# Four early steps of the output projection ahead of a norm's sums, and GpSimd's convolution additions behind the last key write, in a two-layer attention and convolution encoder

## The chip, the cores and the metric

The kernel runs on one core of a Trainium2 chip. The core has five engines that run their own instruction queues, each in order: TensorE (PE, matrix products, with its weight loads shown as PEld), VectorE (DVE), ScalarE (ACT), GpSimd (POOL) and SyncE (SP, which here only issues DMAs). They meet through semaphores. The metric is the device time of one execution in microseconds; lower is better.

## The reference

Two layers of an encoder over 512 tokens of 1024 features, in float32. Only the mixing part in the middle of a layer is touched by the change.

```python
for l in range(DEPTH):                       # 2 layers
    x = x + 0.5 * swiglu(rms_norm(x, ffn1_norm[l]), ...)
    h = rms_norm(x, mix_norm[l])
    p = h @ w_in[l]
    attn = mla_group(p[..., :o_kv], ...)     # 8 heads: q and k per head normalised, 96 wide; block-causal softmax
    conv = conv_group(p[..., o_cv:], ...)    # u = a * sigmoid(g); causal depthwise conv of 31 taps over 512 channels;
                                             # layer norm over the channels; silu
    x = x + jnp.concatenate([attn, conv], axis=-1) @ w_out[l]
    x = x + 0.5 * swiglu(rms_norm(x, ffn2_norm[l]), ...)
    x = rms_norm(x, post_norm[l])
```

## The kernel before

All activations stay in SBUF with features on partitions: x is eight tiles of 128 x 512. Float32 accuracy in the big products comes from splitting each operand into a high and a low part; `mm3` (L170 to L172) issues three matmuls for one product of 128 x 128 weights with 128 x 512 values. The feed-forward parts take most of the time; the change lies in `mix_body`, once per layer.

**Order of the work.** A scheduler places the instructions on the engines from the order in which the code is written; `tc.issue_after(i)` forbids that what follows is placed ahead of i, and `tc.high_priority` brings a block forward. What stands on one engine then runs in that order. Waits between engines are only for data and for buffers.

**Keys.** `keys` takes four tiles of 128 tokens. For each it scales the key of every head by an inverse root that GpSimd works out (`rsqrt`, L189) and writes the two parts of `kn` on VectorE (L820 and L822; L819 scales the factor of the second). `order["keys"]` holds GpSimd's last inverse root. `turn` then transposes queries and keys on TensorE (L848, L853). The first four weight tiles of the output projection (`wo`) are loaded behind `order["keys"]`: their low parts come by a DMA that GpSimd issues (L155).

**Convolution.** Four tiles of 128 channels. Tile 0 and tile 3 are summed on VectorE (L968), 31 taps each. For the other two, ScalarE makes one product per tap into one of four buffers `pr` (L972), and GpSimd adds it to the tile's sum `ys[c]` (L974). For taps from PAUSE = 16 on, and for the second of these tiles, the addition is placed behind `order["keys"]`; these are thirty in a layer. Part of the third tile's taps run on TensorE (L676).

**Attention.** For each head: scores on TensorE (L872), row maxima on VectorE (L876), exponentials on ScalarE (L880), transposes of the probabilities (L895), copies out of PSUM (L898), and for each pair of heads the value products (L917) and their scaling (L920), which `split` makes into an operand of the output projection (L177, L178). ScalarE's exponentials and its products for the convolution are in one queue.

**The norm and the output projection.** The four channel tiles are summed, centred (L1001), squared on ScalarE (L200, L203) and added up on VectorE (L207). TensorE forms the sums per token (`sums`, L214), VectorE and GpSimd make the inverse root, and TensorE spreads it over the partitions (`spread`, L233). Only then are the convolution's tiles scaled (L1016), put through silu (L1018) and split (L177, L178). TensorE needs them as operands 4 to 7 of the projection; operands 0 to 3 are the four pairs of heads. So products with the heads' operands are put around sums and spread as early steps, a step being one operand for one of four output tiles, three matmuls:

```python
steps = [(m, k) for m in range(WOG) for k in range(3)] + [(m, 3) for m in range(WOG)]
...
early_steps(0, EA, heads[H - 1][EARLY])
...
early_steps(EA, EB, sums)
early_steps(EB, len(steps), spreading)
```

With EA = 2 and EB = 6 two of the sixteen steps may come behind the last head's scores, four behind the sums, and ten behind the spread.

Of the kernel before, what the change touches and what calls it, by code (L numbers as in the profile page):

```python
# [12 lines left out]
ALU = mybir.AluOpType  # L13
# [7 lines left out]
NT = S // P  # L21
H = 8
DN = 64
DR = 32
DQ = DN + DR
# [25 lines left out]
GLUP = 0  # L51
EARLY = "s"
PRELOAD = 1
EA = 2
EB = 6
WOG = 4
CHAIN = 400
WAKE = 10
# [20 lines left out]
def encoder_kernel(ctx: ExitStack, tc: tile.TileContext, xT, consts, vecs, rgain, wgu1, wd1, wdq1,  # L79
# [11 lines left out]
    def nm(s):  # L91
        uid[0] += 1
        return f"{s}{uid[0]}"
# [4 lines left out]
    def tmp(w=S, dt=FP):  # L98
        return tmps.tile([P, w], dt, tag="t", name=nm("t"))
# [13 lines left out]
    def tiny(tag, w, dt=FP):  # L113
        return small.tile([P, w], dt, tag=tag, name=nm(tag))

    V, A, G, T = nc.vector, nc.scalar, nc.gpsimd, nc.tensor
# [15 lines left out]
    minus_half = cpool.tile([P, H], FP, name="minus_half")  # L132
# [10 lines left out]
    def vv(l, name):  # L143
        o, w = VOFF[name]
        return vec[:, l, o:o + w]

    def load_w(src, w, kind=""):
        raw = wpool.tile([P, WC], FP, tag="raw", name=nm("raw"), bufs=3)
        nc.sync.dma_start(out=raw[:, :w], in_=src)
        hi = wpool.tile([P, WC], FR, tag="wh", name=nm("wh"))  # L150
        order["cast"] = A.copy(hi[:, :w], raw[:, :w]).ins  # L151
        lo = low()
        if kind == "sum":
            A.activation(lo[:, :w], raw[:, :w], AF.Copy, scale=-1.0)
            G.dma_start(out=lo[:, :w], in_=src, accum_op=ALU.add)  # L155
            return hi, lo
        (G if kind in POOLW.split() else V).tensor_tensor(lo[:, :w], raw[:, :w], hi[:, :w].bitcast(FP),  # L157
                                                          ALU.subtract)
        return hi, lo
# [4 lines left out]
    order = {}  # L164
# [22 lines left out]
    def rsqrt(y, ve):  # L187

        return G.tensor_tensor(y, ve, minus_half[:, 0:y.shape[1]], ALU.pow).ins  # L189
# [439 lines left out]
    def mix(l, gx, norm, done):  # L629
        with tc.tile_pool(name="k", bufs=4) as kpool:  # L630
            mix_body(kpool, l, gx, norm, done)

    def mix_body(kpool, l, gx, norm, done):
        u, order = [], {}
# [53 lines left out]
        kn = kpool.tile([P, NT, H, DQ], FP, tag="kn", name=nm("kn"), bufs=1)  # L688
# [109 lines left out]
        def up_kv(w, t, n=S):  # L798

            ts_ = slice(t * P, (t + 1) * P)  # L800
            ps = bank()
            for k in range(2):
                cs = slice(k * n, (k + 1) * n)
                mm3(ps, ckT[k][0][:, ts_], ckT[k][1][:, ts_], w[0][:, cs], w[1][:, cs], k == 0, k == 1)
            return ps

        def keys():
            wk = load_w(wkv[l, 0], WC, "uk")
            for t in range(NT):
                ps = up_kv(wk, t)  # L810
                A.copy(kn[:, t, :, 0:DN], ps.rearrange("p (h d) -> p h d", h=H))
                j = tmp()
                A.activation(j, ps, AF.Square)
                V.tensor_reduce(ssk[:, t], j.rearrange("p (h d) -> p h d", h=H), axis=AX.X, op=ALU.add)
                V.tensor_scalar(ssk[:, t], ssk[:, t], ckc[:, t:t + 1], None, ALU.add)
                sck = small.tile([P, H], FP, tag="sck", name=nm("sck"))
                order["keys"] = rsqrt(sck, ssk[:, t])
                scp = small.tile([P, H], FP, tag="scp", name=nm("scp"))
                V.tensor_scalar(scp, sck, ratio[:, t:t + 1], None, ALU.mult)  # L819
                V.tensor_tensor(kn[:, t, :, 0:DN], kn[:, t, :, 0:DN],  # L820
                                sck[:, :, None].to_broadcast([P, H, DN]), ALU.mult)
                V.tensor_tensor(kn[:, t, :, DN:DQ], cke[:, t, None, :].to_broadcast([P, H, DR]),  # L822
                                scp[:, :, None].to_broadcast([P, H, DR]), ALU.mult)


        first = groups([wcv[l, 0], wcv[l, 1]], gx)
# [157 lines left out]
        def early_steps(a, b, behind_):  # L984
            with tc.issue_after(behind_):
                for m, k in steps[a:b]:
                    if k == 0:
                        early.append(bank())
                    group(early[m], wo[m], at, (k,), KD)

        early_steps(0, EA, heads[H - 1][EARLY])
        st = Stats()
# [14 lines left out]
        if PRELOAD:  # L1007
            with behind(heads[H - 1]["exps"]):
                A.activation(tiny("pre", 1), ysum[:, 0:1], AF.Silu)
        early_steps(EA, EB, sums)  # L1010
        early_steps(EB, len(steps), spreading)
        lg, lb = vv(l, "lg"), vv(l, "lb")
# [283 lines left out]
```

## Time and profile before

| | us |
|---|---|
| three runs | 1794.69, 1797.07, 1797.32 (median 1797.07) |
| profiled execution, its own time | 1794.2 |
| its span, first to last instruction | 1792.4 |
| PE busy | 1778.5 (99%) |
| DVE busy | 1493.5 (83%) |
| ACT busy | 1093.8 (61%) |
| POOL busy | 382.1 (21%) |
| PE's wait for L207 ahead of the sums, both layers | 2.8 |
| PE's wait for the last keys (L822), both layers | 1.1 |

The granted TensorE clock is 1.00 throughout. In the first layer the keys are written from about 432 to 444 us of the span, attention runs from 445 to about 507, sums and spread stand at 508 and 512; the second layer repeats it some 888 us later. A row of a timeline gives the start, the length, the engine, the line, the operation, its output and inputs, how often it stands there in a row, and in brackets the idle time of the engine ahead of it and what ended it. In a row with several instructions the length is that from the start of the first to the end of the last.

### The profile page before, as it was taken

To read this page: it belongs to the slowest core of one execution; us is meant where nothing else is said; L and a number is where in the kernel's file an instruction comes from. 1 tells how busy PE (TensorE), PEld (TensorE's weight loads), DVE (VectorE), ACT (ScalarE), POOL (GpSimd) and SP (SyncE) were. 2 spreads that over 40 slices of the span, in tenths; PEclk is the share of its full clock that TensorE was granted. 3 is DMA by queue.
4 is the path that set the end of the run, shared out by engine and by line. 5 is a ranking of instruction groups with operands and counts; after the bars stand their busy time and mean duration, and the time that the engine had idled before them with its cause. 6 is when DMAs were issued, how large, how long until landed. Compare 5 with 4: busy or idle time off the path is not lost.

```text
span 1792.4 us, 29441 instructions
## 1 busy us (share of the span) xinstructions
PE 1778.5 (99%) x11430; PEld 1579.1 (88%) x11430; DVE 1493.5 (83%) x2309; ACT 1093.8 (61%) x1699; POOL 382.1 (21%) x313
## 2 busy tenths in 40 slices
PE   9999999999999999999999999999999999999998
PEld 7899999888678899999888999998976788999997
DVE  7898988689965989898779989876999568989883
ACT  5565756467853575756645757564778435756564
POOL 1000000248722000000310000002585310000002
PEclk9999999999999999999999999999999999999999
DMA  5657575324213466665426575743260126575742
GB/s 170 171 131 182 136 178 123 109 84 127 68 28 96 124 166 162 153 160 131 124 65 171 123 194 122 193 114 111 81 157 21 52 79 170 130 185 131 183 117 74
DMA packets 71947, 228.28 MB, mean 127 GB/s; under 512 B 8448, under 2 KB 9600, under 8 KB 71808
## 3 DMA queue, kind: packets, MB, share of 16 engines
q1 hardware_dynamic: 55536, 171.87, 30.5%
q0 software_dynamic: 16128, 54.53, 18.2%
q8 instruction: 89, 1.46, 0.3%
q14 instruction: 50, 0.41, 0.1%
q10 hardware_dynamic: 144, 0.00, 0.0%
HBM read 222.19 MB, written 2.10 MB: 125 GB/s over the span
## 4 chain that ended last, share of the span: by engine, by line
PE 90%; DVE 6%; ACT 1%; issue 1%; DMA 1%; POOL 0%; SPq 0%; ACTq 0%; DVEq 0%
PE ps L170 24%; PE ps L171 23%; PE ps L172 23%; PE ps L389 11%; PE ps L390 6%; DVE cv L968 1%; DVE mx L876 1%; DMA raw<-in_wgu 1%; PE ps L917 1%; DVE r L898 0%; PE ps L895 0%; PE ps L214 0%; DVE r L855 0%; PE ps L676 0%; DVE wl L262 0%
## 5 line engine op out<-in xcount | busy, mean ns | idle before, releaser
L171 PE MATMUL ps<-r,wh 128*128 128x256 f32 (+1 forms) x2556 | 812.9, 319 | 0.1
L170 PE MATMUL ps<-r,wh 128*128 128x256 f32 (+1 forms) x2556 | 811.0, 320 | 1.1 <-ACT wh L151 0.5
L172 PE MATMUL ps<-r,wl 128*128 128x256 f32 (+1 forms) x2364 | 755.3, 321 | 0.0
L170 PEld LDWEIGHTS ps<-r,wh 128*128 128x128 f32 x2556 | 483.8, 189 | 45.6 <-ACT wh L151 3.7
L171 PEld LDWEIGHTS ps<-r,wh 128*128 128x128 f32 x2556 | 484.6, 190 | 36.4 <-DVE r L178 1.5
L172 PEld LDWEIGHTS ps<-r,wl 128*128 128x128 f32 x2364 | 448.2, 190 | 33.8
L389 PE MATMUL ps<-xj,wh 128*128 128x512 f32 x864 | 303.8, 391 | 0.0
L151 ACT CAST wh<-raw 128x1024 fp32r<-128x1024 f32 (+3 forms) x148 | 132.6, 901 | 216.9 <-PE ps L171 135.3
L260 ACT CAST wh<-fr 128x1024 fp32r<-128x1024 f32 (+1 forms) x160 | 157.8, 986 | 103.8 <-DVE fr L426 49.3
L406 POOL DMA_DIRECT2D ls<-in_wgu x72 | 62.5, 868 | 734.5 <-ACT ls L405 525.0
L157 DVE TENSOR_TENSOR wl<-raw,wh 128x1024 fp32r<-128x1024 f32 (+3 forms) x132 | 141.2, 1077 | 91.0 <-ACT wh L151 90.3
L262 DVE TENSOR_TENSOR wl<-fr,wh 128x1024 fp32r<-128x1024 f32 (+1 forms) x160 | 181.8, 1136 | 20.1 <-ACT wh L260 20.1
L389 PEld LDWEIGHTS ps<-xj,wh 128*128 128x128 f32 x864 | 161.4, 188 | 30.1
L390 PE MATMUL ps<-xj,ls 128*128 128x256 f32 x576 | 161.3, 280 | 0.0
L974 POOL TENSOR_TENSOR y<-y,pr 128x495 f32<-128x495 f32 (+29 forms) x90 | 121.7, 1353 | 46.4 <-ACT pr L972 41.0
L260 ACT CAST wh<-raw 128x1024 fp32r<-128x1024 f32 (+1 forms) x100 | 98.1, 981 | 45.2 <-PE ps L171 24.5
L262 DVE TENSOR_TENSOR wl<-raw,wh 128x1024 fp32r<-128x1024 f32 (+1 forms) x100 | 113.3, 1133 | 14.2 <-ACT wh L260 13.8
L390 PEld LDWEIGHTS ps<-xj,ls 128*128 128x128 f32 x576 | 108.3, 188 | 0.0
L405 ACT ACTIVATE ls<-fr 128x1024 fp32r<-128x1024 f32 (+1 forms) x56 | 56.1, 1002 | 75.9 <-PE ps L390 42.8
L207 POOL TENSOR_TENSOR r<-r,t 128x512 f32<-128x512 f32 x45 | 73.3, 1638 | 136.5 <-ACT t L203 136.2
L968 DVE SCALAR_TENSOR_TENSOR cv<-m,vec,cv 128x511 f32<-128x511 f32 (+14 forms) x120 | 87.8, 732 | 3.8 <-ACT cv L964 2.2
L406 POOL DMA_DIRECT2D ls<-in_wdq x32 | 27.6, 863 | 262.1 <-ACT ls L405 262.1
(257 smaller groups left out, 2919.1 us busy)
## 6 DMA issues: line engine op xcount, KB each, us to landing
fr<-in_wgu SPq DMA_DIRECT2D x112, 512.0 KB, 4.3
ls<-in_wgu POOLq DMA_DIRECT2D x72, 512.0 KB, 6.3
raw<-in_wgu SPq DMA_DIRECT2D x62, 512.0 KB, 4.6
fr<-in_wdq SPq DMA_DIRECT2D x48, 384.0 KB, 5.0
ls<-in_wdq POOLq DMA_DIRECT2D x32, 384.0 KB, 4.8
raw<-in_wd SPq DMA_DIRECT2D x32, 384.0 KB, 3.2
raw<-in_wd SPq DMA_DIRECT2D x32, 256.0 KB, 2.8
raw<-in_wcv SPq DMA_DIRECT2D x16, 512.0 KB, 3.6
```

The costliest lines, as they stand in the source:

```text
L151: order["cast"] = A.copy(hi[:, :w], raw[:, :w]).ins
L157: (G if kind in POOLW.split() else V).tensor_tensor(lo[:, :w], raw[:, :w], hi[:, :w].bitcast(FP), ALU.subtract)
L170: T.matmul(o, lh, rh, start=first, stop=False, skip_group_check=free)
L171: T.matmul(o, lh, rl, start=False, stop=False, skip_group_check=free)
L172: order["mm"] = T.matmul(o, ll, rh, start=False, stop=last, skip_group_check=free).ins
L260: A.copy(hi[:, :w], src[:, :w])
L262: order["lo"] = V.tensor_tensor(lo[:, :w], src[:, :w], hi[:, :w].bitcast(FP), ALU.subtract).ins
L389: T.matmul(o, w[0][:, c], both, start=start and k == 0, stop=False, skip_group_check=True)
L390: last = T.matmul(o[:, 0:HS], w[1][:, c], both[:, 0:HS], start=False, stop=k == 3, skip_group_check=True).ins
L406: G.dma_start(out=lo[:, :n], in_=w, accum_op=ALU.add)
L968: V.scalar_tensor_tensor(acc[:, s:], u[c][:, :S - s], tap(k), acc[:, s:], ALU.mult, ALU.add)
L974: order["conv"] = G.tensor_tensor(ys[c][:, s:], ys[c][:, s:], pr[:, s:], ALU.add).ins
```

## The change

`EA` goes from 2 to 4 and `EB` from 6 to 8: four early steps may be placed ahead of the sums, four again between sums and spread, and eight behind the spread. In `keys`, a new product of one column follows the loop over the tiles on GpSimd: it reads the last column of `kn` of the last tile and writes a buffer of one column. `order["keys"]` now names this product, so that the weight loads and the thirty additions are placed behind it. Lines behind L822 move by two: the additions are L976 in the changed kernel, the last heads' scaling L922.

```diff
-EA = 2
-EB = 6
+EA = 4
+EB = 8
...
                 V.tensor_tensor(kn[:, t, :, DN:DQ], cke[:, t, None, :].to_broadcast([P, H, DR]),
                                 scp[:, :, None].to_broadcast([P, H, DR]), ALU.mult)
+            order["keys"] = G.tensor_tensor(tiny("pre", 1), kn[:, NT - 1, H - 1, DQ - 1:DQ], minus_half[:, 0:1],
+                                            ALU.mult).ins
```

The three places of the programs that the prediction rests on are the sums on VectorE, the sums on TensorE, and the first additions on GpSimd. On GpSimd, ahead of the additions (y) behind the last key scale (sck), it stood before:

```order
L189 TENSOR_TENSOR sck_4559<-ssk_3863,minus_half 128x8
L155 DMA wl_5393<-in_wout 128x1024
L974 TENSOR_TENSOR y_3848<-y_3848,pr_5496 128x496
L155 DMA wl_5400<-in_wout 128x1024
L974 TENSOR_TENSOR y_3848<-y_3848,pr_5499 128x495
```

and now:

```order
L189 TENSOR_TENSOR sck_4559<-ssk_3863,minus_half 128x8
L824 TENSOR_TENSOR pre_4565<-kn_3856,minus_half 128x1
L155 DMA wl_5395<-in_wout 128x1024
L155 DMA wl_5402<-in_wout 128x1024
L976 TENSOR_TENSOR y_3848<-y_3848,pr_5498 128x496
L976 TENSOR_TENSOR y_3848<-y_3848,pr_5501 128x495
```

The new product stands ahead of two weight loads and of the additions. On VectorE, where the squares of the convolution's channels (m) are added and the last heads' output (t) is scaled, it stood before:

```order
L207 TENSOR_TENSOR m_4633<-m_4633,m_3846 128x512
L920 TENSOR_TENSOR t_5383<-ps_5374,t_5372 128x512
L207 TENSOR_TENSOR m_4633<-m_4633,m_4058 128x512
L178 TENSOR_TENSOR r_5386<-t_5383,r_5385 128x512
L221 TENSOR_SCALAR vtok_5642<-cv_5643 128x4
```

and now:

```order
L207 TENSOR_TENSOR m_4635<-m_4635,m_3846 128x512
L207 TENSOR_TENSOR m_4635<-m_4635,m_4058 128x512
L922 TENSOR_TENSOR t_5385<-ps_5376,t_5374 128x512
L178 TENSOR_TENSOR r_5388<-t_5385,r_5387 128x512
L221 TENSOR_SCALAR vtok_5651<-cv_5652 128x4
```

The last addition of squares stands ahead of the scaling. On TensorE, from the last value product (ps_5374, now ps_5376) over the sums (L214) to the next steps, before:

```order
L917 MATMUL ps_5374<-r_5346,m_4801 64x128
L214 MATMUL cv_5643<-ones,m_4633 128x1 x4
L170 MATMUL ps_5619<-r_5357,wh_5391 128x512
L171 MATMUL ps_5619<-r_5358,wh_5391 128x512
L172 MATMUL ps_5619<-r_5357,wl_5393 128x512
```

and now:

```order
L919 MATMUL ps_5376<-r_5348,m_4803 64x128
L170 MATMUL ps_5621<-r_5359,wh_5393 128x512
L171 MATMUL ps_5621<-r_5360,wh_5393 128x512
L172 MATMUL ps_5621<-r_5359,wl_5395 128x512
L171 MATMUL ps_5631<-m_5159,wh_5400 128x512
L172 MATMUL ps_5631<-m_5158,wl_5402 128x512
L214 MATMUL cv_5652<-ones,m_4635 128x1 x4
```

The two steps stand between the value products and the sums, but for their sixth matmul (L170 of ps_5631), which stands ahead of the value products. The orders on PE, DVE, ACT and POOL around the attention differ in further places, and SyncE's is the same.

## The prediction

> **What bounds the kernel now.** I read the page first: the span, the busy times and the chain.
>
> ```profile
> span 1792.4 us, 29441 instructions
> PE 1778.5 (99%) x11430; PEld 1579.1 (88%) x11430; DVE 1493.5 (83%) x2309; ACT 1093.8 (61%) x1699; POOL 382.1 (21%) x313
> PE 90%; DVE 6%; ACT 1%; issue 1%; DMA 1%; POOL 0%; SPq 0%; ACTq 0%; DVEq 0%
> ```
>
> TensorE (PE) is busy for 1778.5 of 1792.4 us and carries 90% of the chain. No multiplication leaves the program, so a gain comes out of the 13.9 us in which TensorE stands still, or out of a stretch where another engine paces it. Next, the windows of the first layer's attention and of what follows it (columns behind the length: PE, its weight loads, DVE, ACT, POOL, the granted clock, DMA):
>
> ```profile
> 445.00:500.00 55.00, 54.48 (x446) 35.34 (x446) 54.02 (x101) 47.32 (x117) 37.06 (x30) 1.00 0.26 65
> 500.00:530.00 30.00, 28.62 (x138) 21.34 (x135) 16.76 (x25) 14.33 (x23) 5.07 (x3) 1.00 0.02 4
> ```
>
> From 445 to 500 VectorE (DVE) works 54.02 of 55.00 us and paces the stage. From 500 to 530 TensorE has 1.38 us without work. The view of TensorE's waits (total, times, longest) names that gap, and one more:
>
> ```profile
> PE cv L214 <- DVE m L207: 2.8, 2, 1.4
> PE ps L853 <- DVE kn L822: 1.1, 2, 0.9
> ```
>
> The change touches both: 2.8 us ahead of the two norms' sums and 1.1 us ahead of the transposes of the last keys, 3.9 us or 0.22% of the span.
>
> **Part 1: four steps ahead of the sums.** The timeline of the first layer around the sums:
>
> ```profile
> 504.38 2.37 PE L917 MATMUL ps<-r,m 128*64 128x512 f32 x14
> 508.13 1.05 PE L214 MATMUL cv<-ones,m 128*128 128x1 f32 x8 [1.38 <-DVE m L207]
> 516.93 0.39 PE L170 MATMUL ps<-r,wh 128*128 128x512 f32 x1
> ...
> 517.61 0.39 PE L170 MATMUL ps<-r,wh 128*128 128x512 f32 x1
> 504.08 1.48 DVE L207 TENSOR_TENSOR m<-m,m 128x512 f32<-128x512 f32 x2
> 506.79 0.69 DVE L920 TENSOR_TENSOR t<-ps,t 128x512 f32<-128x512 f32 x1 [1.23 <-PE ps L917]
> 507.39 0.68 DVE L207 TENSOR_TENSOR m<-m,m 128x512 f32<-128x512 f32 x1
> 504.80 0.63 ACT L203 ACTIVATE m<-m 128x512 f32<-128x512 f32 x1 [0.51 <-DVE m L207]
> ```
>
> TensorE ends its last value products at 506.75 and has nothing until the sums, which need the third addition of squares (507.39). That addition is queued behind L920, which waits for those value products. A step is three matmuls, and steps start 0.68 us apart (516.93, 517.61); two more of them are 1.36 us, almost exactly the gap.
>
> On VectorE the orders in the section on the change show that the third addition now stands ahead of the scaling of the last heads' output (L920, now L922), and so ahead of the wait. Its square is there at 504.80 + 0.63 = 505.43, the additions before it end at 505.56, so it ends near 506.2. On TensorE, by the orders there, five of the six matmuls now stand between value products and sums; the sixth moved ahead of the value products. The sums start at 506.75 + 6 x 0.227 = 508.11, where they started before, and the addition they need is 1.9 us early. Behind them:
>
> ```profile
> 509.22 0.16 DVE L221 TENSOR_SCALAR vtok<-cv 128x4 f32<-128x4 f32 x1 [0.37 <-PE cv L214]
> 510.53 0.69 DVE L229 TENSOR_TENSOR m<-cst,rtok 128x512 f32<-128x512 f32 x1 [1.14 <-POOL rtok L189]
> 511.91 1.02 PE L233 MATMUL cv<-m,ones 128*128 128x512 f32 x2
> 515.76 0.69 DVE L178 TENSOR_TENSOR r<-m,r 128x512 fp32r<-128x512 f32 x1 [0.31 <-ACT r L177]
> 518.90 0.68 DVE L178 TENSOR_TENSOR r<-m,r 128x512 fp32r<-128x512 f32 x1
> 519.65 1.07 PE L170 MATMUL ps<-r,wh 128*128 128x512 f32 x4
> ```
>
> Between sums and spread (L233) again stand four steps, 2.7 us, so the spread stays near 511.91; its operand is ready at 511.22, 0.7 us early. Behind the spread stand eight steps instead of ten: TensorE comes to the first convolution operand at 519.65 - 1.36 = 518.29. That operand is split by 516.45, 1.8 us early; the last of four by 519.58, and twelve matmuls (2.7 us) of the first fill the time. Nothing new is late. Part 1 is worth 2 x 1.36 = **2.7 us**; 2.8 at most, by the wait's row, and nothing if another wait takes its place.
>
> **Part 2: GpSimd's additions behind the last key write.** VectorE's key writes, GpSimd (POOL) beside them, and who waited:
>
> ```profile
> 435.48 0.75 DVE L822 TENSOR_TENSOR kn<-cke,scp 128x256 f32<-128x256 f32 x2
> 436.76 0.22 DVE L819 TENSOR_SCALAR scp<-sck,ratio 128x8 f32<-128x8 f32 x1
> 437.50 2.35 DVE L822 TENSOR_TENSOR kn<-cke,scp 128x256 f32<-128x256 f32 x1
> 439.77 1.94 DVE L819 TENSOR_SCALAR scp<-sck,ratio 128x8 f32<-128x8 f32 x1
> 442.23 1.46 DVE L822 TENSOR_TENSOR kn<-cke,scp 128x256 f32<-128x256 f32 x1
> 437.34 0.91 POOL L155 DMA_DIRECT2D wl<-in_wout  x1
> 438.00 1.55 POOL L974 TENSOR_TENSOR y<-y,pr 128x496 f32<-128x496 f32 x1
> 445.34 5.87 POOL L974 TENSOR_TENSOR y<-y,pr 128x492 f32<-128x492 f32 x4
> 452.06 0.88 POOL L155 DMA_DIRECT2D wl<-in_wout  x1 [0.85 <-ACT wl L154]
> 443.74 0.32 PE L853 MATMUL ps<-cst,kn 128*96 128x128 f32 x1 [0.88 <-DVE kn L822]
> ```
>
> Ahead of GpSimd's DMA issue and additions two key writes took 0.75 us together; beside them one took 2.35 and one 1.46, and a scaling of 8 columns took 1.94 instead of 0.22. The 2.35 us write ends at 439.85, just behind the addition that ends at 439.55. The Trainium skill, "SBUF — State Buffer", section "Who interferes with whom", has it that a VectorE instruction with two SBUF inputs and a GpSimd one that reads SBUF shut each other out, whoever issues second waiting in full. The trace agrees with it, by 439.85 against 439.55. By that rule the additions may only hand their hold on to later VectorE work with two SBUF inputs; part 2 would then be worth nothing and the sum 2.7 us. On GpSimd, by the order shown with the change, queued behind the new product, which waits for VectorE, are the DMAs of the output weights and all thirty additions of the layer that are left. Unstretched, the last key write ends near 437.50 + 0.38 + 0.74 + 0.38 = 439.0 instead of 443.69 (0.74: from the scaling's start at 436.76 to the write at 437.50). The product is bounded by GpSimd's smallest arithmetic:
>
> ```profile
> L842 POOL TENSOR_SCALAR gqs<-vec 96x1 f32<-96x1 f32 x2 | 0.6, 291 | 12.3 <-DMA vec<-in_vecs 12.2
> L1166 POOL TENSOR_TENSOR gc<-vec 128x8 f32<-128x8 f32 x1 | 0.6, 567 | 0.1
> 464.39 14.29 POOL L974 TENSOR_TENSOR y<-y,pr 128x495 f32<-128x495 f32 x11
> 467.01 1.23 POOL L974 TENSOR_TENSOR y<-y,pr 128x493 f32<-128x493 f32 x1
> 469.42 0.75 ACT L972 ACTIVATE pr<-m,vec 128x489 f32<-128x489 f32 x1
> 483.12 1.60 POOL L996 TENSOR_TENSOR m<-m,y 128x512 f32<-128x512 f32 x1
> 497.95 0.64 DVE L997 TENSOR_TENSOR m<-m,m 128x512 f32<-128x512 f32 x1
> 503.36 0.40 PE L172 MATMUL ps<-m,wl 128*128 128x512 f32 x1
> ```
>
> With 0.3 to 0.6 us for it and two DMA issues at 0.66 (437.34 to 438.00), additions begin near 440.8, 2.8 us later than 438.00. The 0.85 us idle ahead of the fourth DMA takes part of that back, so from 452 on GpSimd is some 2 us late. That hides at its end: its last sum is done at 484.72 and wanted at 497.95 (L997). The first weights that its DMAs bring are used at 503.36 (wl), over 60 us after the issue. In between it has four product buffers: ScalarE's product for 489 (469.42) reuses the one that the addition for 493 freed at 468.24, a lead of 1.18 us. So up to 0.8 us a layer can reach ScalarE, and behind its products stand the exponentials. Against it stand the 1.1 us of TensorE's wait for keys. Part 2 lies between -1.6 and +1.1 us over both layers; I take **+0.5**, nearer to the wait's row, because that wait goes for certain while the lead is used up only in places.
>
> **Sum.** 2.7 + 0.5 = 3.2 us. The profiled execution took 1794.2 us (span 1792.4 and 1.8 around it), so it would take 1791.0. The runs' median is 2.9 above it; the four times of before (1794.2, 1794.69, 1797.07, 1797.32) have a mean of 1795.8, and from that I forecast 1792.6 us. About 0.2%, 3.6 us of the median, is what a measurement can tell from no change.
>
> **Rivals.** *GpSimd becomes late (slower).* In the order now, additions meet other VectorE work. If the thirty take 1.47 us each (5.87 for four at 445.34) instead of 1.30 (14.29 for eleven at 464.39), GpSimd ends 30 x 0.17 + 2 = 7.1 us late; less the lead of 1.18, some 5.9 us of ScalarE's exponentials stall in each layer, 11.8 - 2.7 = 9.1 us slower, near 1804.9. It decides from a delay of 1.18 + 1.36 = 2.5 us on, 0.02 us an addition by this count, more where ScalarE's products stand further back in its order. Against it: the late additions ran at 1.30 beside the same VectorE work. *The gap only moves.* If spread or convolution operands come 1.4 us later, TensorE waits there instead and part 1 is worth nothing: 1795.8 - 0.5 = 1795.3. For it speak only 0.7 us of slack ahead of the spread. *More.* VectorE paces attention and is relieved of (2.35 - 0.38) + (1.94 - 0.22) + (1.46 - 0.38) = 4.8 us a layer; the rule named above says so too. If one more microsecond a layer carries through: 1790.6.
>
> **Chances.** Forecast 0.60, GpSimd late 0.12, gap moves 0.15, more 0.13. The four times spread over 3.1 us, so of the forecast three quarters fall beyond 0.2% (below 1793.5): faster 0.45 + 0.13 = 0.58; the rest of it and the moved gap, 0.30, are within; slower 0.12. The range 1789.5 to 1797.0 takes the forecast, the larger gain and the moved gap with that spread, and leaves out the late GpSimd and a little of the edges.
>
> **What would show it.** No wait of TensorE for L207 ahead of the sums, and none of 1 us behind the spread; the last L822 at 0.4 us and no wait of L853; first additions near 2.8 us later and ScalarE's products not waiting for them between 452 and 480. It is wrong if ScalarE's products wait for GpSimd there, or if the sums wait for VectorE.

## The result, and the profile after

The changed kernel takes 1790.38 us (median of 6 runs, 1789.9 to 1792.67), the kernel before 1797.19 us (6 runs, 1794.69 to 1798.79). The ratio is 0.9968 with a 95% interval of 0.9958 to 0.9979: 5.7 us faster, between 3.8 and 7.5. The forecast was 1792.6 us, 3.2 us below its own base of 1795.8.

The page after, span and busy times (the changed kernel's first profiled execution, 1792.67 us):

```profile
span 1790.6 us, 29441 instructions
PE 1778.9 (99%) x11430; PEld 1580.5 (88%) x11430; DVE 1484.7 (83%) x2309; ACT 1094.0 (61%) x1699; POOL 383.4 (21%) x315
```

Its waits of TensorE, as they were read before (total, times, longest):

```profile
PE ps L170 <- ACT wh L1114: 1.1, 1, 1.1
PE ps L131 <- DVE ones L127: 1.1, 1, 1.1
PE ps L874 <- ACT r L882: 1.0, 2, 0.5
PE ps L170 <- ACT wh L151: 0.8, 2, 0.5
PE ps L676 <- DMA r<-m: 0.5, 1, 0.5
```

The rows for the sums (2.8 us) and for the last keys (1.1 us) are gone. Two new rows stand in the list: the first weights of the program (L1114), which the change does not touch, and, in one layer, copies of the convolution's input (r<-m) that the taps on TensorE (L676) need. The timeline around the sums:

```profile
506.08 2.37 PE L919 MATMUL ps<-r,m 128*64 128x512 f32 x14
509.65 0.95 PE L214 MATMUL cv<-ones,m 128*128 128x1 f32 x8
513.33 1.02 PE L233 MATMUL cv<-m,ones 128*128 128x512 f32 x2
505.55 2.27 DVE L207 TENSOR_TENSOR m<-m,m 128x512 f32<-128x512 f32 x3
508.49 0.69 DVE L922 TENSOR_TENSOR t<-ps,t 128x512 f32<-128x512 f32 x1 [0.66 <-PE ps L919]
511.94 0.69 DVE L229 TENSOR_TENSOR m<-cst,rtok 128x512 f32<-128x512 f32 x1 [1.15 <-POOL rtok L189]
```

The three additions of squares stand together ahead of VectorE's wait and end at 507.82, 1.8 us ahead of the sums; the spread's operand is there at 512.63, 0.7 us ahead of 513.33. No row of TensorE has a bracket. At the keys, VectorE and GpSimd:

```profile
438.19 0.41 DVE L822 TENSOR_TENSOR kn<-cke,scp 128x256 f32<-128x256 f32 x1
438.52 0.22 DVE L819 TENSOR_SCALAR scp<-sck,ratio 128x8 f32<-128x8 f32 x1
439.26 0.41 DVE L822 TENSOR_TENSOR kn<-cke,scp 128x256 f32<-128x256 f32 x1
439.75 0.19 POOL L824 TENSOR_TENSOR pre<-kn,minus_half 128x1 f32<-128x1 f32 x1 [1.67 <-DVE kn L822]
441.17 3.23 POOL L976 TENSOR_TENSOR y<-y,pr 128x496 f32<-128x496 f32 x2
485.88 1.27 POOL L998 TENSOR_TENSOR m<-m,y 128x512 f32<-128x512 f32 x1
```

The last key write ends at 439.67 instead of 443.69, GpSimd stands 1.67 us, its additions start at 441.17 (438.00 before), and its last sum ends at 487.15 (484.72 before).

### The profile page after: what moved, and what is told of

Same layout as the page of the kernel before. It is cut to its first block, busy times and chain, and to the rows that moved or that the text cites. A ratio compares the mean times of both kernels' runs of the same rounds, so it can differ in the third digit from the quotient of the medians.

```text
span 1790.6 us, 29441 instructions
## 1 busy us (share of the span) xinstructions
PE 1778.9 (99%) x11430; PEld 1580.5 (88%) x11430; DVE 1484.7 (83%) x2309; ACT 1094.0 (61%) x1699; POOL 383.4 (21%) x315
## 4 chain that ended last, share of the span: by engine, by line
PE 82%; DVE 3%; ACT 1%; DMA 0%; issue 0%; SPq 0%; ACTq 0%; DVEq 0%
PE ps L170 21%; PE ps L172 21%; PE ps L171 21%; PE ps L389 9%; PE ps L390 5%; PE ps L874 1%; PE ps L919 1%; PE ps L897 1%; DVE cv L970 1%; PE ps L912 0%; PE ps L676 0%; DVE mx L878 0%; PE ps L214 0%; DVE wl L262 0%; PE ps L233 0%; DMA r<-m 0%
## 5 line engine op out<-in xcount | busy, mean ns | idle before, releaser
L170 PE MATMUL ps<-r,wh 128*128 128x256 f32 (+1 forms) x2556 | 811.3, 321 | 2.6 <-ACT wh L1114 1.1
L171 PE MATMUL ps<-r,wh 128*128 128x256 f32 (+1 forms) x2556 | 812.9, 319 | 0.0
L170 PEld LDWEIGHTS ps<-r,wh 128*128 128x128 f32 x2556 | 483.7, 189 | 47.5 <-ACT wh L151 3.5
L171 PEld LDWEIGHTS ps<-r,wh 128*128 128x128 f32 x2556 | 484.5, 190 | 36.6 <-issue 1.9
L976 POOL TENSOR_TENSOR y<-y,pr 128x495 f32<-128x495 f32 (+29 forms) x90 | 120.6, 1343 | 45.9 <-ACT pr L974 40.6
```

The lines of the kernel that those rows point to most:

```text
L170: T.matmul(o, lh, rh, start=first, stop=False, skip_group_check=free)
L171: T.matmul(o, lh, rl, start=False, stop=False, skip_group_check=free)
L976: order["conv"] = G.tensor_tensor(ys[c][:, s:], ys[c][:, s:], pr[:, s:], ALU.add).ins
```

## The experiments

Where the figures of one execution are added up below, they are TensorE's idle time in three stretches of each layer: the keys, the attention, and from the last value products to the first output. The views of the windows give it as length minus PE's busy time (columns: PE, PEld, DVE, ACT, POOL, clock, DMA). Before:

```profile
425.00:445.00 20.00, 19.12 (x94) 15.84 (x92) 19.34 (x32) 9.60 (x12) 19.74 (x17) 1.00 0.66 165
445.00:504.00 59.00, 58.48 (x465) 37.42 (x464) 57.28 (x106) 49.91 (x122) 37.06 (x30) 1.00 0.24 60
504.00:530.00 26.00, 24.62 (x114) 19.25 (x114) 13.51 (x20) 11.74 (x18) 5.07 (x3) 1.00 0.03 5
1313.00:1333.00 20.00, 19.78 (x96) 16.39 (x95) 19.34 (x31) 9.83 (x12) 18.23 (x13) 1.00 0.68 169
1333.00:1391.00 58.00, 57.04 (x458) 35.89 (x457) 55.77 (x105) 48.92 (x120) 36.09 (x29) 1.00 0.23 56
1391.00:1417.00 26.00, 24.62 (x115) 19.25 (x114) 13.52 (x21) 11.81 (x18) 4.57 (x3) 1.00 0.01 1
```

Keys 0.88 + 0.22 = 1.10 us, attention 0.52 + 0.96 = 1.48, sums 1.38 + 1.38 = 2.76: 5.34 us in all (5.33 by unrounded sums).

**The four steps alone** (steps_only), **the product behind the keys alone** (keys_only), **both and before again** (both_again, before_again, no edit).

```diff
# steps_only, against before
-EA = 2
-EB = 6
+EA = 4
+EB = 8
# keys_only, against before
+            order["keys"] = G.tensor_tensor(tiny("pre", 1), kn[:, NT - 1, H - 1, DQ - 1:DQ], minus_half[:, 0:1],
+                                            ALU.mult).ins
```

> The four steps ahead of the sums alone (EA 4, EB 8, no product behind the keys). Theory (the prediction's part 1): the wait of TensorE for L207 of 1.38 us a layer is gone, no other appears in the same stretch, the wait for the last keys (0.9 and 0.2 us) stays: 2.7 us less than before. Rival 1 (the gain lies mostly in the relief of VectorE at the keys): here 0 to 1.5 us less. Rival 2 (the measured 6 us is one interaction: the steps only pay once the keys are early): here less than 1.4 us, with a new wait at the spread or the convolution operands.

> The product behind the key loop alone (EA 2, EB 6 as before). Theory (part 2): wait for the last keys gone, additions some 3 us later, the gap ahead of the sums stays at 1.38 us a layer; 0.5 us less than before, between 1.1 less and 1.6 more. Rival 1: TensorE reaches attention over 1 us a layer earlier and keeps it: 3 to 4 us less. Rival 3 (TensorE, come earlier, waits for the shifted copies r<-m at L676, as 1.5 us of the first layer in the changed kernel's trace): the gain at the keys is given back there, 0 to 1 us less.

> The changed kernel itself once more, for a second profile. Theory: 3.2 to 6 us less than before; if the wait at L676 in the first layer (1.5 us) is a matter of how the transfers happened to fall, it is 0 to 0.3 us in one of the two layers here; if it belongs to the change, it is again over 1 us in the first.

> The kernel before once more, for a second profile. Theory: the same two waits (2.8 and 1.1 us) and a span of 1792 to 1796 us; what differs from the first profile lies outside the mixing stage (head, feed-forward parts) and tells how much of a difference between two profiled executions is not the change's: 1 to 3 us. Rival: the span differs by over 1 us within the attention stage, so that single traces of before are no base for terms of under 1 us there.

Measured against before (median 1796.62 us): steps alone 1792.23 us, ratio 0.9972 (0.9961 to 0.9983), 5.0 us less; keys alone 1794.67 us, 0.9986 (0.9977 to 0.9995), 2.5 us less; both 1791.68 us, 0.9968 (0.9956 to 0.9981). The six stretches of both, in its second profile:

```profile
425.00:445.00 20.00, 20.00 (x98) 16.81 (x97) 16.19 (x34) 8.90 (x12) 17.56 (x16) 1.00 0.59 152
445.00:504.00 59.00, 58.33 (x463) 37.44 (x463) 55.53 (x106) 51.31 (x123) 39.06 (x32) 1.00 0.27 65
504.00:530.00 26.00, 26.00 (x120) 20.42 (x120) 14.03 (x20) 13.28 (x21) 5.38 (x3) 1.00 0.03 9
1313.00:1333.00 20.00, 20.00 (x98) 16.78 (x97) 14.57 (x31) 9.68 (x12) 16.24 (x12) 1.00 0.64 154
1333.00:1391.00 58.00, 57.31 (x459) 36.33 (x459) 55.37 (x105) 49.83 (x122) 37.43 (x31) 1.00 0.23 58
1391.00:1417.00 26.00, 26.00 (x121) 20.73 (x118) 14.12 (x19) 13.79 (x21) 6.01 (x3) 1.00 0.06 16
```

Keys 0, attention 0.67 + 0.69 = 1.36, sums 0: 3.98 us less than before. VectorE in attention is 0.4 to 1.8 us less busy than before, not more. The parts nearly add up: with the steps alone 2.18 us are left (keys 1.10, attention 1.08, sums 0), with the keys alone 4.10 (0, 1.33, 2.76), so 3.16 and 1.24 us less, 4.40 together. Most of the 0.4 us beyond 3.98 lies in the second layer's attention: before stands still there for 0.96 us, and each of the three others for 0.56 to 0.69, so that both parts count it. One row of each names what stays, the first from the steps alone, the second from the keys alone:

```profile
PE ps L853 <- DVE kn L822: 1.1, 2, 0.9
PE cv L214 <- DVE m L207: 2.8, 2, 1.4
```

The wait for the copies r<-m does not belong to every execution: it is not in the second profile of the same kernel, where the taps take 3.60 us in one piece. It came back, with 0.8 us, in two of the later profiles (late14 and late40); before never had it. In the first profile the taps were broken:

```profile
455.99 1.06 PE L676 MATMUL ps<-r,m 128*32 128x512 f32 x6
457.55 3.58 PE L676 MATMUL ps<-r,m 128*32 128x512 f32 x26 [0.50 <-DMA r<-m]
```

From 455.99 to 461.13 they take 5.14 us, 1.5 us more than in one piece.

The second profile of before has the same two waits, took 1794.48 us, and has 5.31 us of idle time in the six stretches where the first has 5.33: for these stretches single traces of before are a base to a few hundredths. No rival on the parts holds in the traces: the steps bring their 2.76 us without the keys, and the keys alone bring 1.24 us, not 3 to 4, and do not lose them at L676. By the timed runs alone (0.9 to 4.1 us less) the size of the keys' part would be open.

**Three, six and eight steps ahead of the sums** (steps3, steps6, steps8; the keys' product stays).

```diff
# steps3          steps6          steps8
-EA = 4           -EA = 4         -EA = 4
-EB = 8           -EB = 8         -EB = 8
+EA = 3           +EA = 6         +EA = 8
+EB = 7           +EB = 10        +EB = 12
```

> The changed kernel with EA 3 and EB 7: three early steps ahead of the sums in place of four (before: two). Theory (a step fills 0.68 us of the gap): TensorE waits 0.7 us a layer ahead of the sums, 1.4 us slower than the changed kernel. Rival (it is the third addition of squares, placed ahead of VectorE's wait, that brings the gain, not the steps): the sums start 0.7 us earlier than in the changed kernel and no wait is left; the same as the changed kernel within 0.5 us or better.

> The changed kernel with EA 6 and EB 10. By the prediction's chain the two further steps put sums, spread and convolution operands off by 1.36 us; the first operand was split 1.8 us ahead of its use and is still 0.5 us early: the same as the changed kernel within 0.3 us in the layers' stretches. Rival (the slack ahead of the first operand was overrated, as the 0.6 us a layer that eight steps lost against the 0.9 expected may be underrated): 0.5 us or more a layer lost.

> The changed kernel with EA 8 and EB 12: eight early steps ahead of the sums in place of four, four again between sums and spread, four behind it. The prediction's chain: four steps are 2.7 us, so sums, spread and convolution operands come 2.7 us later, the first operand at 516.45 + 2.7 = 519.2 where TensorE wants it at 518.3; 0.9 us a layer are lost, 1.8 us slower than the changed kernel, with a wait of TensorE for L178 or ScalarE's split there. Rival (the sums need no room, a step is worth the same wherever it stands): the same within 0.5 us.

Measured: three steps 1792.35 us, 0.9974 (0.9964 to 0.9985); six steps 1790.57 us, 0.9965 (0.9952 to 0.9979); eight steps 1792.02 us, 0.9978 (0.9969 to 0.9986). The intervals overlap with that of the changed kernel, so the times alone do not part them; the timelines do. TensorE at the sums with three steps; at the sums and at the first convolution operand (L170, four in a row) with six; and with eight, there with ScalarE's write of that operand's high part (L177):

```profile
507.51 1.05 PE L214 MATMUL cv<-ones,m 128*128 128x1 f32 x8 [0.48 <-DVE m L207]
509.21 0.95 PE L214 MATMUL cv<-ones,m 128*128 128x1 f32 x8
517.85 1.07 PE L170 MATMUL ps<-r,wh 128*128 128x512 f32 x4
511.70 0.95 PE L214 MATMUL cv<-ones,m 128*128 128x1 f32 x8
518.32 0.39 PE L170 MATMUL ps<-r,wh 128*128 128x512 f32 x1
519.25 1.20 PE L170 MATMUL ps<-r,wh 128*128 128x512 f32 x4
522.13 1.07 PE L170 MATMUL ps<-r,wh 128*128 128x512 f32 x4
518.59 0.60 ACT L177 CAST r<-m 128x512 fp32r<-128x512 f32 x1
```

With three steps the third addition of squares stayed behind VectorE's wait, and 0.48 us of the gap are left in each layer (0.7 expected), 0.9 us less than with two: the gap closes with the steps. The fourth step came together with the addition's move ahead of the wait. Whether that move alone, with two steps, would have closed the gap as well was not tried: no run has it. With six nothing waits, as the slack of 1.8 us at the first operand foretold. With eight the first operand is met too late: 0.93 us from the last step to it where steps are 0.68 apart, and 2.88 us to the second where four steps are 2.72; at least 0.4 us a layer lost, less than the 0.9 expected. The reason is in the same trace. VectorE ends the operand's low part (L178) at 519.92, 0.9 us after TensorE could have used it at 519.00, as counted. But the four L170 read only the high part, which ScalarE ends at 519.19, and the low part is first read at 520.29 (L171).

**More delay for GpSimd, and the loads without it** (late14, late40, loads_early; all with four steps).

```diff
# late14 (late40: range(40))
+            for _ in range(14):
-            order["keys"] = G.tensor_tensor(tiny("pre", 1), kn[:, NT - 1, H - 1, DQ - 1:DQ], minus_half[:, 0:1],
-                                            ALU.mult).ins
+                order["keys"] = G.tensor_tensor(tiny("pre", 1), kn[:, NT - 1, H - 1, DQ - 1:DQ], minus_half[:, 0:1],
+                                                ALU.mult).ins
# loads_early
+            order["scales"] = order["keys"]
             order["keys"] = G.tensor_tensor(tiny("pre", 1), kn[:, NT - 1, H - 1, DQ - 1:DQ], minus_half[:, 0:1],
                                             ALU.mult).ins
...
-        with tc.issue_after(order["keys"]):
+        with tc.issue_after(order["scales"]):
             wo = [load_w(wout[l, m], WC, "sum") for m in range(WOP)]
```

> The changed kernel with fourteen of the small products in place of one, so that GpSimd's weight loads and additions start 13 x 0.15 to 0.2 = 2.0 to 2.6 us later still. Theory A (the prediction's count of the lead: four product buffers give ScalarE 1.18 us; what GpSimd is late beyond that stalls ScalarE's products and the exponentials behind them): GpSimd is 4 to 4.6 us late in all, 2.8 to 3.4 us a layer reach ScalarE, 3 to 6 us slower than the changed kernel. Theory B (GpSimd waits for ScalarE's products anyway, and so makes up a late start): no product of ScalarE waits, the same as the changed kernel within 1 us.

> The same with forty small products: additions 6 to 8 us later than in the changed kernel. Theory A: 5 us or more a layer reach ScalarE, over 8 us slower than the changed kernel. Theory B: what GpSimd can make up is the time that it stands waiting for products ahead of 452 us (0.9 and 1.0 us before its fourth weight load, some 1 to 2 us more in the conv's first half), so that of this delay too some 4 us a layer come through: 4 to 9 us slower. If it is the same as the changed kernel within 1 us, the lead that the prediction counted is no limit at all.

> The changed kernel with the weight loads of the output projection behind GpSimd's last inverse root, as before, and only the additions behind the last key write: the two loads that waited are issued 2 to 3 us earlier. Theory C (the key writes were stretched by the additions): key writes stay at 0.41 us, the wait for the last keys stays gone; the same as the changed kernel within 1 us. Rival D (the descriptors of the loads stretch VectorE as well): one key write stays over 1 us, and up to 1 us a layer is given back. Rival E (in the first profile of the changed kernel TensorE waits 1.5 us for the shifted copies r<-m, which run beside the loads that are now later): loads earlier, less collision, up to 0.8 us better on average.

Measured: fourteen products 1793.29 us, 0.9983 (0.9974 to 0.9992); forty 1793.52 us, 0.9988 (0.9979 to 0.9996); loads early 1791.7 us, 0.9973 (0.9963 to 0.9983). The products and GpSimd's own waits in the first layer, fourteen first, then forty:

```profile
439.27 2.04 POOL L825 TENSOR_TENSOR pre<-kn,minus_half 128x1 f32<-128x1 f32 x14 [1.67 <-DVE kn L822]
POOL y L977 <- ACT pr L975: 1.1, 1, 1.1
439.59 5.75 POOL L825 TENSOR_TENSOR pre<-kn,minus_half 128x1 f32<-128x1 f32 x40 [1.67 <-DVE kn L822]
POOL y L977 <- ACT pr L975: 1.5, 2, 1.2
```

With forty products the additions come 5.6 us later (5.75 against 0.19), and GpSimd still waits for ScalarE, never ScalarE for GpSimd. 11 us of delay in two layers cost some 2 to 4 us by the timed runs (0.9988 and 0.9968; medians measured at different times 1.8 to 3.1 apart). The traces show less: TensorE stands still for 2.27 us with fourteen products and 2.45 with forty, 0.9 and 1.1 more than in both_again, and 0.8 of that is the wait for r<-m. Theory A, the count of the lead, falls. Theory B is nearer: the price of forty lies at or below its 4 to 9 us, and that of fourteen, by the medians 1.6 to 2.9 us, is above its 1 us. Five of the eleven runs of forty (1793.5 to 1797.3 us) read a granted clock of 0.998 or less, so a part of its price goes with the clock (see the sum below). One caution: with the longer delay the scheduler also placed ScalarE's products later in its queue, so these runs show what a delay costs with the order that goes with it; a delay in an unchanged order was not tried.

With the loads early, GpSimd's DMA issue lies beside VectorE's key write and nothing is stretched, while ScalarE's products wait for GpSimd (in before this row had 1.1 us, in the changed kernel it is not in the list):

```profile
437.77 0.91 POOL L155 DMA_DIRECT2D wl<-in_wout  x1
437.92 0.41 DVE L822 TENSOR_TENSOR kn<-cke,scp 128x256 f32<-128x256 f32 x1
438.26 0.22 DVE L819 TENSOR_SCALAR scp<-sck,ratio 128x8 f32<-128x8 f32 x1
ACT pr L975 <- POOL y L977: 2.6, 1, 2.6
```

So it is the additions that stretch, not the loads (theory C, rival D falls). Rival E's gain does not show: TensorE's idle time in the six stretches is 2.47 us, 1.1 more than in both_again.

**The taps one head later** (taps_later) and **before a third time** (before_third, no edit).

```diff
-PSTEP = 3
+PSTEP = 4
```

> The changed kernel with the convolution's taps on TensorE (L676) one head later, which gives the shifted copies r<-m some 5 us more. Theory (TensorE, come earlier by the keys, meets copies that are late in some executions: 1.5 us in one of the two layers of the changed kernel's first profile): no wait for r<-m, and 0 to 1 us better on average than the changed kernel. Rival (the sum of the taps is then late for ScalarE's bias and GpSimd's second tile): a wait for y or a later last sum on GpSimd, 0.5 us or more slower.

> The kernel before a third time, for its profile. Both profiled executions so far (1794.2 and 1794.48 us) lie at the low end of its timed runs (median 1796.1), with the head 1 us quicker than any changed kernel's and a granted clock of 1.000. If that is chance, this one has a head or a clock like the others' and a time of 1795 to 1797; if it belongs to the kernel, again 1794.2 to 1794.5 with a quick head.

Measured: taps later 1791.79 us, 0.9976 (0.9966 to 0.9986). No wait for r<-m, but more for the exponentials, all in attention (2 times and 1.0 us in the changed kernel):

```profile
PE ps L874 <- ACT r L882: 2.4, 6, 0.5
```

TensorE's idle time in the two attention stretches is 1.52 + 1.59 = 3.11 us against 1.36. The taps are work that TensorE does while it would wait for exponentials; later they cover less. The theory of a gain falls, for a reason that its rival did not name either.

Before took 1794.72 us in its third profile, with the same waits. Three profiled executions of before (1794.2, 1794.48, 1794.72) lie at the low end of the timed runs beside them (1794.19 to 1799.42, median 1796.21 beside the third). Each of the three reads a granted clock of 1.000.

## Why the prediction was right, and where a term was mis-sized

**Part 1, 2.7 us: right, step by step.** The gap of 1.38 us a layer is filled (2.76 us less in the windows), the third addition moved ahead of the wait and is 1.8 us early (1.9 forecast), the spread's operand 0.7 us early (0.7 forecast). The slack at the first convolution operand was tested by dose: six steps cost nothing, eight do. Its size was put 0.5 us too low: eight steps should have lost 0.9 us a layer and lost about 0.4, because the count went by the operand's low part, and the first four products read the high part alone.

**Part 2, +0.5 us: sign right, size too small.** The key writes went back to 0.41 us, the wait of 1.10 us went, and attention gave nothing of it back (1.48 to 1.36 us): 1.24 us in the trace of keys_only, just above the term's range of -1.6 to +1.1. The step that failed is "So up to 0.8 us a layer can reach ScalarE". The delay came as counted (additions 3.2 us later, of which 0.7 us is this execution's later arrival at the keys; GpSimd's last sum 2.4 us later), but no product of ScalarE behind the keys waited for GpSimd, in either layer. The lead of 1.18 us was read in the order of before; in the order that goes with the change ScalarE's products stand elsewhere. The first one behind the keys, for 492, starts at 445.14 instead of 439.58, and the second tile's product for 489 at 473.23 (L974) instead of 469.42. This order, which the prediction had not counted, is the likely reason that nothing of the 1.1 us was lost; the delay in the old order was not tried.

**The rivals.** GpSimd late, from 2.5 us of delay on: it does not hold in the orders that were run, since late40 has 5.6 us more and costs a fraction. The gap only moves: refuted by steps_only and steps6. More from VectorE's relief: the groups of the stretched lines (count, total us and mean ns), before and then after, show that the relief is real:

```profile
L822 DVE TENSOR_TENSOR kn<-cke,scp 128x256 f32<-128x256 f32 x8 | 9.1, 1161 | 0.0
L819 DVE TENSOR_SCALAR scp<-sck,ratio 128x8 f32<-128x8 f32 x8 | 5.2, 652 | 1.3 <-POOL sck L189 1.3
L822 DVE TENSOR_TENSOR kn<-cke,scp 128x256 f32<-128x256 f32 x8 | 3.2, 416 | 0.0
L819 DVE TENSOR_SCALAR scp<-sck,ratio 128x8 f32<-128x8 f32 x8 | 1.8, 223 | 1.3 <-POOL sck L189 1.3
```

That is 9.3 us less for VectorE over both layers, 9.6 forecast. It was not handed on to later VectorE work either (windows of attention: 57.28 to 55.53 and 55.77 to 55.37 us). But only the 1.1 us in which TensorE waited for it came through: in attention VectorE is busy for 94 to 97% of the time, yet TensorE's idle time there hardly changed. The prediction's reading that VectorE paces that stage was wrong by its own row: from 445 to 500 TensorE is busy for 54.48 of 55.00 us, more than VectorE's 54.02. The two attentions of before hold 1.48 us of idle time of TensorE in all, so one more microsecond in each layer was hardly there to be had. The Trainium skill, "SBUF — State Buffer", section "Who interferes with whom", says that a VectorE instruction with at most one SBUF input (outside a mode that takes both ports) does not contend with GpSimd. The traces agree: beside the additions of the changed kernel L646 and L942, with one input from PSUM, take 0.69 us each (442.85; 2.06 for three at 447.63), while L652, of the same size but with both inputs in SBUF, takes 1.32 us (446.39) instead of the 0.68 that it takes ahead of the additions (436.85). L652 was stretched in before too (1.33 us at 446.12), so this is no hold that was handed on. That the reads of PSUM are why nothing was handed on is argued, not tried. Nor do the rows of the prediction show which of two such instructions waits: the write of 2.35 us began at 437.50, ahead of the addition at 438.00, and was still the one that was stretched most.

**The sum, and what stays open.** The traces account for 4.0 us (both_again) and, with the broken taps, 3.5 us (after), against 3.2 forecast. The timed runs give 5.7 us, 3.8 to 7.5, which holds 4.0. The spans differ by less, 1790.0 against 1792.4: the head of the program is part of it (PE's busy time in the first 12 us, before and both_again):

```profile
0.00:12.00 12.00, 10.89 (x46) 9.26 (x47) 7.28 (x17) 8.56 (x13) 0.20 (x4) 1.00 0.86 291
0.00:12.00 12.00, 9.78 (x43) 8.09 (x44) 6.83 (x17) 8.05 (x13) 0.20 (x4) 1.00 0.84 283
```

TensorE waits 1.2 us there for the first weights. All three profiles of before lack that wait and all eleven others have it, 0.3 to 1.4 us long, though no instruction of the head was edited. Why is open.

Most of what the timed runs gain beyond the traces goes with TensorE's granted clock, for which the prediction had no term. Its mean is on record for each of the 63 timed runs of before that were taken beside the experiments, and the time goes with it: 1794.7 us on average at 1.000 (10 runs), 1796.2 at 0.999 (21), 1796.7 at 0.998 (20) and 1798.1 at 0.997 (12). The eleven timed runs of the changed kernel read 1.000 (three, 1790.6 us on average) or 0.999 (eight, 1791.3). A reading of 0.999 can come without a fall in the middle: in the changed kernel's first profile the clock is 0.50 at the very end (1789 to 1791), where TensorE has no work left. At 1.000 the two kernels are 4.1 us apart, by three runs of the one only, and the traces account for 4.0. So the forecast's 3.2 us are to be held against these 4; as far as these runs tell, most of the rest of the 5.7 goes with falls of the clock in runs of before, which no term of the forecast held. The profiled executions of before, all at 1.000, lie some 2 us below its timed runs for the same reason; why all three were at 1.000 is not known.

What brings the falls is not shown. The gap ahead of the sums is a candidate: the one fall that a trace holds (the last section) begins about 1.5 us behind it. None of the 51 timed runs of kernels with four or more steps and no further delay of GpSimd reads below 0.999, against 5 of 11 with the keys alone. But late40, with four steps, reads 0.998 or less in 5 of 11 too.

The forecast's base, the mean of the four times, counted the profiled execution of before as the fourth; it lies 0.3 to 1.4 us below the medians of before that were measured later.

## What to carry to other kernels

Fill a gap with exactly the work it holds, and check the slack of every consumer behind it: here two more steps filled the gap of 1.38 us, two further ones were free, and four met the next operand late. When a wait is taken away by delaying another engine's queue, look at the order that the scheduler then makes, not only at the lead in the old one. An engine that is over 90% busy need not be the limit: 9 us of relief on VectorE brought TensorE little more than the 1.1 us that it had stood waiting. When medians and traces disagree, compare the granted clock of the timed runs with that of the profiled ones.

## What the runs showed of the hardware

The granted clock can fall for a few microseconds in one execution, and a single trace then misprices a stage. In the profile of keys_only the window behind the sums of the first layer:

```profile
508.00:512.00 4.00, 4.00 (x17) 3.34 (x18) 1.55 (x3) 0.84 (x1) 1.03 (x1) 0.68 0.00 0
```

PE is busy throughout at a clock of 0.68; 4 us at 0.68 are some 1.3 us lost, and the 8 us behind them, at 0.95, lose another 0.4. Matmuls that start 0.23 us apart elsewhere start 0.42 us apart from 509.45 to 512.84. TensorE had stood still for 1.38 us just before, from 506.61 to 507.99, and is busy in between. The sums of the second layer, behind the same gap, and the same stretch of the other kernels show 1.00. Of the fourteen profiles only this one has a mean clock of 0.998; the others read 0.999 or 1.000.
